# Hybrid decoder trunk: when a block's DMA transposes are issued and when its halves are joined

## The chip, the cores and the metric

The kernel runs on one core of one Trainium2 chip. The metric is device time in microseconds of one execution. A core has five engines that work side by side, each with its own queue of instructions: TensorE (PE in the profile; PEld is its loading of stationary operands), VectorE (DVE), ScalarE (ACT), GpSimd (POOL) and SyncE (SP). DMAs are issued here by SP, by POOL (those that add to what stands at their destination) and a few by ACT; sixteen DMA engines of the core carry them out.

## The reference

Two layers over 512 tokens of width 1024 in float32. Each has a SwiGLU feed-forward part (ffn) of width 2816, a token mixer (windowed attention beside a short convolution, not touched here), and a second ffn:

```python
x = x + 0.5 * swiglu(rms_norm(x, ffn1_norm[l]), ffn1_wg[l], ffn1_wu[l], ffn1_wd[l])
...
x = x + jnp.concatenate([attn_out, conv_out], axis=-1) @ w_out[l]
x = x + 0.5 * swiglu(rms_norm(x, ffn2_norm[l]), ffn2_wg[l], ffn2_wu[l], ffn2_wd[l])
...
def swiglu(h, w_gate, w_up, w_down):
    return (jax.nn.silu(h @ w_gate) * (h @ w_up)) @ w_down
```

A final RMSNorm follows.

## The kernel before

**Precision.** Every operand of a matmul is split into two halves of reduced precision, `hi` and `lo`; a product is made of three matmuls (hi by hi, lo by hi, hi by lo). For weights, `split` does this: ScalarE casts `raw` to `wh` (L214), VectorE subtracts to get `wl` (L215). There are three buffers each of `wh` and `wl`, and `need_split` runs two splits ahead of the matmuls.

**Pairs.** An ffn is a list of stages (`FIRST`, `INNER` or `LAST`). A stage "w" (`winograd2`) computes the gate and up products of 512 hidden columns, called a block here, with seven products in place of eight (a Strassen-like scheme, `CHAINS`). It has seven steps; each consumes two weight tiles of 512 KB and runs 24 matmuls of 128 x 512 (`stream`, L816). I call such a stage a pair and count its steps from 0 in the code, from the first in the text. In the first ffn the last such stage is a narrower form of 256 columns ("u", `winograd`). A pair needs ten weight tiles; four of them are sums of two matrices, loaded by SP and completed by an accumulating DMA of POOL (L209). There are eight buffers `raw` for 512 KB tiles, loaded ahead in the order of the plan; a load waits on SP's queue until its buffer is free, and everything behind it on that queue waits too.

**Share stages.** After the pairs, a stage "s" (`share`) multiplies the activations of two blocks by `wd`, again seven products for eight; an ffn has two such stages, and the block of its last pair, which is in neither, is turned on TensorE. In it POOL also sums two weight tiles by DMA (L281). In the very last ffn a closing stage "e" stands in place of the second share (its tiles end in `_e`).

**Crossing.** The activations `ups` leave a pair with tokens on the partitions, four tiles of 128 x 512 float32, and the share stage needs the hidden columns there. The blocks listed in `blocks` (four in each of the four ffn, sixteen in all) are turned by DMA: an object `Crossing` is put on the list `crossing` at the end of its pair, and its `step` is called once at the end of each step of the pairs that follow (`turns`). For each of four token tiles ScalarE copies the float32 words apart into their upper and lower 16-bit halves (`halves`, L1090), and SP issues a DMA transpose of 2-byte elements into `turned` (L1091). Later `join` (L1105) has ScalarE put the two halves together again, four copies of 128 x 1024 16-bit words, into `raw_a`, from which the operands of the share stage are made. A join needs all four transposes of its block. `join` stands behind the latest cast in ScalarE's order (`issue_after`).

When: with `n` the count of steps since the block was made, a block's transposes go at n = 0 to 3, one per step, and its joins at n = 8 and 9, two each, that is in the second and third step of the pair after the next. The last block of an ffn (`b == max(blocks)`) has `first = 3`: its transposes go in the fourth to seventh step of the last pair, and the first share stage joins it in its fourth step (`joined`). `turned` and `raw_a` come from a pool of four buffers (`g8`), `halves` from a pool of fourteen (`g2`).

The order on an engine's queue is the program's order, rearranged by a scheduler; the transposes share SP's queue with the weight loads (L197).

Of the kernel before, what the change touches and what calls it, by code (L numbers as in the profile page):

```python
# [25 lines left out]
NT = S // P  # L26
# [46 lines left out]
def trunk_kernel(  # L73
# [35 lines left out]
    def g2(name, dt=F32, shape=(P, S)):  # L109
        return work.tile(list(shape), dt, tag="g2", bufs=14, name=name)  # L110

    def g8(name, dt=F32R, shape=(P, 2, 2, S)):
        return work.tile(list(shape), dt, tag="g8", bufs=4, name=name)
# [778 lines left out]
    def ffn(norm, stages, after=None, late=None):  # L892
# [43 lines left out]
        def winograd(b, between):  # L936
# [9 lines left out]
            def keep(what, m, src):  # L946
                if m == 0:
                    kept[what] = g2(f"{what}_{name}", F32, (P, 2, H))
                nc.scalar.copy(kept[what][:, m, :], src)

            for step, (acc, operand, start) in enumerate(CHAINS):
                _, wh, wl = take_split()
                xh, xl = norm.forms[operand]
# [5 lines left out]
                for m in range(2):  # L959
# [27 lines left out]
                    if step == 6:  # L987
                        nc.scalar.activation(gate[:, t2], out, AF.Silu)
                        nc.vector.tensor_mul(up, up, gate)
                        split(hi[:, m, :], lo[:, m, :], up)  # L990
                turns(step)
                between(step)
            acts[b] = (hi, lo)

# [72 lines left out]
        class Crossing:  # L1067
# [2 lines left out]

            def __init__(self, b, name, ups):
                self.b, self.name, self.ups = b, name, ups

                self.first = 3 if b == max(blocks) else 0
                self.steps = 0
                self.to = None

# [3 lines left out]
            def step(self):  # L1081

                n = self.steps
                self.steps += 1
                t = n - self.first
                if t == 0:
                    self.to = g8(f"turned_{self.name}", U16, (P, 2, NT, S))
                if 0 <= t < NT:
                    halves = g2(f"halves{t}_{self.name}", U16, (P, 2, S))
                    nc.scalar.copy(halves, self.words(self.ups[t]))  # L1090
                    nc.sync.dma_start_transpose(  # L1091
                        self.to.rearrange("p a c s -> p (a c) s")[:, :, t * P : (t + 1) * P],
                        halves.rearrange("p a n -> p (a n)"),
                    )
                if n in (8, 9):
                    self.join(*((0, 1), (2, 3))[n - 8])
                return n == 9

            def join(self, *cs):

# [29 lines left out]
        blocks = [b + j for what, b in stages if what in "se" for j in (0, 2)]  # L1130
# [512 lines left out]
```

## Time and profile before

| | |
|---|---|
| median of 3 runs | 1681.74 us (1675.95 to 1684.97) |
| the profiled execution | 1688.44 us, its span 1686.6 us, granted TensorE clock 0.996 |
| VectorE, ScalarE busy in the span | 82%, 64% |
| mean DMA rate | 179 GB/s |
| transposes | 64 |

The span runs from the first to the last instruction. An engine's busy share is a mean over stages with different limits, so the prediction goes by stage. In lines of waits the name after the arrow is who ended the wait; a wait for several is put down to the one that came last.

### The profile page before, as it was taken

How to read it: one execution, taken by the hardware profiler on the slowest of the kernel's cores; microseconds unless marked ns; L12 is line 12 of the kernel's file. 1: busy time of each engine (PE TensorE's matmuls, PEld its weight loads, DVE VectorE, ACT ScalarE, POOL GpSimd, SP SyncE). 2: the span in 40 equal slices, each digit the busy share in tenths (PEclk: the TensorE clock that was granted, in tenths of full speed). 3: DMA queues.
4: the chain of work that ended last, by engine and by line, in shares of the span. 5: the costliest groups of instructions: out<-in, count | busy, mean ns of one | idle time of the engine just before them, and what ended most of it. 6: DMA issues, size and time to landing. Idle time of an engine off the chain costs nothing. (4 is left out here: it accounts for less than half of the span.)

```text
span 1686.6 us, 22112 instructions
## 1 busy us (share of the span) xinstructions
PE 1650.6 (98%) x8140; PEld 1389.9 (82%) x8140; DVE 1381.6 (82%) x1824; ACT 1073.0 (64%) x1425; POOL 212.4 (13%) x188
## 2 busy tenths in 40 slices
PE   9999999999999999989999999999999999999988
PEld 7888889988898878877888778878888988888766
DVE  7987679988899967778898667888788997678887
ACT  6446776466576667757466567764565766777645
POOL 0011111001111111111011111110012111111121
PEclk9999999999999999999999999999999999999999
DMA  8379997831497799898567999985125968998992
GB/s 251 88 189 204 239 215 191 199 88 52 126 226 166 186 191 240 212 169 218 174 138 188 191 216 215 197 222 170 50 63 140 223 138 212 216 216 206 209 252 74
DMA packets 260129, 301.92 MB, mean 179 GB/s; under 512 B 76652, under 2 KB 145332, under 8 KB 260020
## 3 DMA queue, kind: packets, MB, share of 16 engines
q1 hardware_dynamic: 219428, 218.04, 46.2%
q0 software_dynamic: 39872, 81.80, 29.0%
q8 instruction: 64, 1.05, 0.2%
q10 hardware_dynamic: 720, 0.66, 0.1%
q14 instruction: 45, 0.37, 0.1%
HBM read 262.71 MB, written 2.10 MB: 157 GB/s over the span
## 5 line engine op out<-in xcount | busy, mean ns | idle before, releaser
L214 ACT CAST wh<-raw 128x1024 fp32r<-128x1024 f32 (+1 forms) x491 | 511.3, 1046 | 453.2 <-PE x L816 101.4
L215 DVE TENSOR_TENSOR wl<-raw,wh 128x1024 fp32r<-128x1024 f32 (+1 forms) x491 | 593.8, 1219 | 188.7 <-ACT wh L214 187.8
L310 PE MATMUL acc<-xh,wh 128*128 128x512 f32 x424 | 165.8, 392 | 0.0
L311 PE MATMUL acc<-xl,wh 128*128 128x512 f32 x424 | 165.5, 390 | 0.0
L313 PE MATMUL acc<-xh,wl 128*128 128x512 f32 x416 | 162.2, 390 | 0.0
L209 POOL DMA_DIRECT2D raw<-in_ffn_wu_dram x39 | 48.9, 1254 | 403.1 <-DMA raw<-in_ffn_wu_dram 324.5
L311 PEld LDWEIGHTS acc<-xl,wh 128*128 128x128 f32 x424 | 79.7, 188 | 15.9 <-DVE xl L491 0.2
L310 PEld LDWEIGHTS acc<-xh,wh 128*128 128x128 f32 x424 | 79.8, 188 | 15.7
L313 PEld LDWEIGHTS acc<-xh,wl 128*128 128x128 f32 x416 | 78.1, 188 | 16.4
L1105 ACT COPY raw_a<-turned 128x1024 uint16<-128x1024 uint16 x64 | 84.1, 1361 | 0.0
L251 DVE TENSOR_TENSOR raw<-raw,raw 128x1024 f32<-128x1024 f32 x56 | 68.0, 1222 | 19.4 <-DMA raw<-in_ffn_wu_dram 17.3
L209 POOL DMA_DIRECT2D raw<-in_ffn_wg_dram x39 | 48.2, 1248 | 239.2 <-DMA raw<-in_ffn_wu_dram 135.1
L209 POOL DMA_DIRECT2D raw<-in_ffn_wd_dram x34 | 41.0, 1206 | 279.9 <-DMA raw<-in_ffn_wd_dram 139.1
L816 PE MATMUL w<-wl,fb21h 128*128 128x512 f32 x152 | 59.4, 391 | 3.8 <-DVE wl L215 3.8
L816 PE MATMUL x<-wh,ft1h 128*128 128x512 f32 x152 | 59.3, 390 | 1.4 <-ACT wh L214 1.4
L816 PE MATMUL x<-wl,ft1h 128*128 128x512 f32 x152 | 59.8, 394 | 0.8 <-DVE wl L215 0.8
L816 PE MATMUL y<-wl,ft3h 128*128 128x512 f32 x152 | 59.2, 390 | 0.4 <-DVE wl L215 0.4
L816 PE MATMUL w<-wh,fb21h 128*128 128x512 f32 x152 | 59.3, 390 | 0.0
L816 PE MATMUL x<-wh,ft1l 128*128 128x512 f32 x152 | 59.2, 390 | 0.0
L816 PE MATMUL y<-wh,ft3h 128*128 128x512 f32 x152 | 59.2, 390 | 0.0
L816 PE MATMUL x<-wh,ft2h 128*128 128x512 f32 x152 | 59.2, 390 | 0.0
L816 PE MATMUL w<-wh,fb21l 128*128 128x512 f32 x152 | 59.2, 389 | 0.0
(604 smaller groups left out, 4606.1 us busy)
## 6 DMA issues: line engine op xcount, KB each, us to landing
raw<-in_ffn_wu_dram SPq DMA_DIRECT2D x126, 512.0 KB, 4.9
raw<-in_ffn_wd_dram SPq DMA_DIRECT2D x105, 512.0 KB, 5.8
raw<-in_ffn_wg_dram SPq DMA_DIRECT2D x86, 512.0 KB, 5.0
raw<-in_ffn_wu_dram POOLq DMA_DIRECT2D x39, 512.0 KB, 9.7
raw<-in_ffn_wg_dram POOLq DMA_DIRECT2D x39, 512.0 KB, 6.1
raw<-in_w_in_dram SPq DMA_DIRECT2D x36, 512.0 KB, 3.7
raw<-in_ffn_wd_dram POOLq DMA_DIRECT2D x34, 512.0 KB, 8.7
raw<-raw POOLq DMA_DIRECT2D x21, 512.0 KB, 8.0
```

The lines of the kernel that those rows point to most:

```text
L209: nc.gpsimd.dma_start(out=r, in_=rows_of(*more), accum_op=ALU.add)
L214: cast = nc.scalar.copy(hi, raw)
L215: eng.tensor_sub(lo, raw, f32(hi))
L251: nc.vector.tensor_add(a11, a11, s1)
L310: nc.tensor.matmul(acc, hi[:, k, :], rhs[k][0], start=k == first, stop=False)
L311: nc.tensor.matmul(acc, hi[:, k, :], rhs[k][1], start=False, stop=False)
L313: nc.tensor.matmul(acc, lo[:, k, :], rhs[k][0], start=False, stop=k == last)
L816: nc.tensor.matmul(accs[u], x_[:, 2 * h + k, tok], w[:, k, :], start=start and h + k + i == 0, stop=h + k == 2 and i == 2, skip_group_chec ...
L1105: nc.scalar.copy(self.words(raws[self.b][:, c, :]), self.to[:, :, c, :])
```

## The change

The transposes of every block, the last one too, go in the first two steps of the next pair, two in each. A block that is not the last of its ffn is joined in the sixth and seventh step of that same pair, two copies in each; the last block is joined by the first share stage, as before. The attribute `first` goes. Nothing is computed differently, and the loads and splits keep their order among themselves but for two neighbouring loads in the last ffn.

```diff
             def __init__(self, b, name, ups):
                 self.b, self.name, self.ups = b, name, ups
-
-                self.first = 3 if b == max(blocks) else 0
                 self.steps = 0
                 self.to = None
...
                 n = self.steps
                 self.steps += 1
-                t = n - self.first
-                if t == 0:
+                if n == 0:
                     self.to = g8(f"turned_{self.name}", U16, (P, 2, NT, S))
-                if 0 <= t < NT:
+                for t in {0: (0, 1), 1: (2, 3)}.get(n, ()):
                     halves = g2(f"halves{t}_{self.name}", U16, (P, 2, S))
                     nc.scalar.copy(halves, self.words(self.ups[t]))
                     nc.sync.dma_start_transpose(
                         self.to.rearrange("p a c s -> p (a c) s")[:, :, t * P : (t + 1) * P],
                         halves.rearrange("p a n -> p (a n)"),
                     )
-                if n in (8, 9):
-                    self.join(*((0, 1), (2, 3))[n - 8])
-                return n == 9
+
+                if n in (5, 6) and self.b != max(blocks):
+                    self.join(*((0, 1), (2, 3))[n - 5])
+                    return n == 6
+                return False
```

On SP's queue the new order within a pair is: transpose, load, transpose, load, transpose, load, transpose, load; before it was transpose, three loads, transpose, and so on.

## The prediction

> **What bounds the kernel now.** I read the page first, for who is busy, then a table of busy time by stage, then the waits inside the stages that come out too long, then the DMAs in flight there.
>
> ```profile
> span 1686.6 us, 22112 instructions
> PE 1650.6 (98%) x8140; PEld 1389.9 (82%) x8140; DVE 1381.6 (82%) x1824; ACT 1073.0 (64%) x1425; POOL 212.4 (13%) x188
> ```
>
> TensorE sets the time; only its 36 us of idleness, and what it runs slowly, can be won. The table by stage (start and end, length, busy time of each engine with its count, granted clock, DMA share, GB/s) shows where. The boundaries are the first matmuls of the stages.
>
> ```profile
> 580.11:618.19 38.08, 38.08 (x170) 31.54 (x168) 27.88 (x29) 23.77 (x29) 4.84 (x4) 1.00 1.00 186
> 618.19:658.17 39.98, 38.48 (x170) 31.37 (x168) 27.52 (x29) 27.68 (x33) 4.81 (x4) 1.00 0.94 241
> 658.17:696.32 38.15, 38.15 (x169) 31.46 (x168) 27.61 (x29) 27.90 (x33) 4.81 (x4) 1.00 0.93 219
> 696.32:734.40 38.08, 38.08 (x169) 31.54 (x168) 34.41 (x36) 31.72 (x37) 4.82 (x4) 1.00 0.88 161
> 734.40:781.17 46.77, 40.79 (x170) 32.41 (x168) 31.41 (x32) 27.98 (x32) 6.65 (x6) 0.96 0.99 217
> ...
> 956.41:1000.38 43.97, 39.31 (x169) 31.23 (x168) 27.52 (x29) 27.88 (x33) 4.81 (x4) 1.00 1.01 222
> ...
> 1038.54:1077.18 38.64, 38.38 (x169) 31.45 (x168) 35.22 (x36) 31.81 (x37) 4.84 (x4) 1.00 0.87 185
> 1077.18:1117.34 40.16, 38.65 (x169) 31.38 (x168) 31.32 (x32) 28.01 (x32) 6.64 (x6) 1.00 0.96 230
> ...
> 1570.36:1614.46 44.10, 41.08 (x185) 32.84 (x184) 36.41 (x41) 26.92 (x30) 9.17 (x9) 1.00 1.06 263
> ```
>
> A pair of 168 matmuls takes 38.08 us undisturbed (first row). The exceptions: two pairs, each the third of its ffn, are 1.90 and 5.89 us too long, one last pair 0.56. The share stage after a last pair has as many matmuls and is 8.69 and 2.08 too long; the third one also runs 16 transposes, eight in 0.87 us by the chain of waits, which leaves 44.10 - 38.08 - 1.74 = 4.28. One more wait stands at the start of the closing stage:
>
> ```profile
> 1583.98 0.87 PE at L1054 x8
> ...
> 1628.17 0.77 PE L816 MATMUL x_e<-wh,ft2h_e 128*128 128x512 f32 x1 [5.38 <-DVE bias L1259]
> ...
> 1632.07 0.39 PE L816 MATMUL x_e<-wh,ft2h_e 128*128 128x512 f32 x1
> ```
>
> 5.38 us idle, and after it nine matmuls from 1628.17 to 1632.07 in 3.90 us where nine take 9 x 0.227 = 2.04 (38.08 / 168): 7.24 in all. Together 1.90 + 5.89 + 0.56 + 8.69 + 2.08 + 4.28 + 7.24 = 30.6 us. What is late there? For the first of them, by the DMAs in flight:
>
> ```profile
> 604.64 3.25 SPq L1091 DMA_TRANSPOSE turned<-halves  x1
> 603.53 1.20 POOL L209 DMA_DIRECT2D raw<-in_ffn_wu_dram  x1 [19.55 <-DMA raw<-in_ffn_wu_dram]
> 606.19 1.21 POOL L209 DMA_DIRECT2D raw<-in_ffn_wu_dram  x1 [1.46 <-DMA raw<-in_ffn_wu_dram]
> ...
> raw<-in_ffn_wg_dram SPq DMA_DIRECT2D x86, 512.0 KB, 5.0
> raw<-in_ffn_wg_dram SPq DMA_DIRECT2D x2, 512.0 KB, 11.5
> turned<-halves SPq DMA_TRANSPOSE x1, 14.7
> ACT wh L214 <- DMA raw<-in_ffn_wg_dram: 3.6, 1, 3.6
> ```
>
> The block's fourth transpose left between two accumulating loads of POOL and took 14.7 us to land; the two weight loads issued beside it took 11.5 at the median (5.0 over the whole run, the row above), and at 618 to 628 us ScalarE waited 3.6 us for such a load, with TensorE behind it. Transposes that meet no accumulating load are quick; those that do are slow (landing of those issued at 666 to 679, at 720 to 739, at 964 to 974 us):
>
> ```profile
> DMA to landing us min/median/max: 2.7/3.1/3.4
> DMA to landing us min/median/max: 11.2/17.8/19.6
> DMA to landing us min/median/max: 7.9/9.7/11.5
> ```
>
> The second row is the last block's four, just ahead of the share stage that is 8.69 too long; the third lies in the pair that is 5.89 too long.
>
> **The change part by part.** It removes and adds no instruction: 64 transposes, 64 halves copies and 64 joins stay.
>
> ```profile
> L1091 SPq DMA_TRANSPOSE turned<-halves x64: 1231/1233/6863, 124.9 to 1578.3; - x64
> L1090 ACT COPY halves<-u x32: 1027/1044/1076, 123.8 to 1556.4; 128x1024 uint16<-128x1024 uint16 x32
> L1105 ACT COPY raw_a<-turned 128x1024 uint16<-128x1024 uint16 x64 | 84.1, 1361 | 0.0
> ```
>
> *Transposes of the twelve earlier blocks.* In the pair from 580.11 the fourth left at 604.64, 24.5 us in, 1.1 us after the accumulating load. In the new order all four stand among the first four loads of the SP queue in the pair, the last just ahead of the fourth. Their copies follow the first step (5.44 us) and the second (10.9): with two silus of 0.6 and two copies of 1.04 after it, the last is ready some 14 to 15 us in (estimate), 8 us before the first accumulating load at 23.4 us in. A transpose alone lands in 3.1 us, so it is gone by then. I take the 1.90, 5.89 and 0.56 as won: 8.3 us. Bounds: 0 if the meeting only moves, 8.35.
>
> *The same for the last block.* Its transposes leave in the first two steps of the last pair rather than from the fourth on: some 8 to 15 us into 696.32 to 734.40, not 720 to 739. The DMA share of this stage is only 0.88, so there is room. The share stages lose 8.69 + 2.08 + 4.28 = 15.05; part of it is the second half of the stage, whose loads wait for buffers behind the sum on POOL. I take 0.8 of it, 12 us; bounds 0 and 15.05.
>
> *Closing stage.* Its 7.24 us end in loads that queue at a DMA share of 1.06; they start earlier when the share stage's loads do, but TensorE comes earlier too. I take half, 3.6; bounds 0 and 7.24.
>
> *Against it, in the first ffn:*
>
> ```profile
> 235.25 1.19 POOL L209 DMA_DIRECT2D raw<-in_ffn_wd_dram  x1 [11.70 <-DMA raw<-in_ffn_wd_dram]
> 240.88 1.20 POOL L209 DMA_DIRECT2D raw<-in_ffn_wd_dram  x1 [4.45 <-DMA raw<-in_ffn_wd_dram]
> ...
> 247.97 3.94 SPq L1091 DMA_TRANSPOSE turned<-halves  x2
> ```
>
> The last pair there is the narrow form. Its transposes go from 248 and later to about 239 to 246 us, onto these two accumulating loads. One such meeting cost 1.9 in the row at 618.19 and, with a second, 5.89: I take 2; bounds 0 and 5.9.
>
> *SP queue.* Three transposes now pass ahead of loads that they stood behind, 3 x 1.23 us of issue. The delayed loads are the end of the same pair's weights and the next pair's first, needed 15 us and more later by TensorE: nothing, and 3.7 us a pair if that cover were gone.
>
> *ScalarE.* The joins move from the second and third step to the sixth and seventh, two per step, between the casts there:
>
> ```profile
> 1488.63 1.05 ACT L214 CAST wh<-raw 128x1024 fp32r<-128x1024 f32 x1 [1.67 <-PE y L816]
> 1491.35 1.05 ACT L214 CAST wh<-raw 128x1024 fp32r<-128x1024 f32 x1 [1.67 <-PE x L816]
> 1492.93 0.60 ACT L1038 ACTIVATE gate<-x 128x512 f32<-128x512 f32 x1 [0.53 <-PE x L816]
> 1494.07 1.06 ACT L214 CAST wh<-raw 128x1024 fp32r<-128x1024 f32 x1 [0.54 <-PE x L816]
> 1495.03 0.58 ACT L1038 ACTIVATE gate<-x 128x512 f32<-128x512 f32 x1
> 1496.64 1.23 DVE L251 TENSOR_TENSOR raw<-raw,raw 128x1024 f32<-128x1024 f32 x1 [1.77 <-DMA raw<-in_ffn_wu_dram]
> 1498.39 1.22 DVE L215 TENSOR_TENSOR wl<-raw,wh 128x1024 fp32r<-128x1024 f32 x1
> ```
>
> The idle times in brackets are the room. In the new order two joins of 1.36 precede the first cast, which ends at 1490.7; the second is on time, to 1492.4; join to 1493.8, gate to 1494.4, join to 1495.7, gate to 1496.3, and the cast of 1494.07 ends at 1497.4. Its wl starts in the trace only at 1498.39, since VectorE stands behind a sum (L251) that waits for an accumulating load, so the wl is no later than now: done at 1499.6, where TensorE's second step begins at 1494.09 + 5.44 = 1499.5 and wants wl with its third matmul, at 1500.0. That 0.4 us is what is late next: behind this wl queue the following wl, then TensorE. Nothing by this count; I take 2 us over the twelve blocks, bounds 0 and 12 (one us each). A join also waits for the last landing: 15 + 3.1 us in, wanted at 29.
>
> Sum: 8.3 + 12 + 3.6 - 2 - 2 = 20 us off the profiled execution's 1688.44 (span 1686.6, the rest around it): 1668.4. The median before is 1681.74, 6.7 lower, so the runs shown have fewer of these waits; with the won waits scaled by (30.6 - 6.7) / 30.6 it is 1681.7 - (23.9 x 0.78 - 4) = 1667.
>
> **Rivals.** *The meeting moves to the head of the pair (slower).* The other two accumulating loads of a pair are issued near its start, and now two transposes follow at once:
>
> ```profile
> 658.97 1.20 POOL L209 DMA_DIRECT2D raw<-in_ffn_wg_dram  x1 [8.57 <-DVE p L1039]
> 661.08 1.20 POOL L209 DMA_DIRECT2D raw<-in_ffn_wg_dram  x1 [0.90 <-DVE raw L251]
> ...
> 962.79 2.48 POOL L209 DMA_DIRECT2D raw<-in_ffn_wg_dram  x2 [17.12 <-DMA raw<-in_ffn_wu_dram]
> ```
>
> For it: where these loads went out at 962.79, the transpose issued at 964 to 965 met them and landed in 7.9 us or more (third landing row). Against: at 658.97 and 661.08 they were in time, the transposes issued from 666 on land in 3.1, and without the meeting at 24 us into the pair before, the loads come earlier. The price is what a pair lost by one meeting, 1.90, or half of 5.89, which had two, 2.9; at 2.3 and 16 blocks 37 us against 24 won: 1688 + 13 = 1701. It decides once more than ten blocks meet (24 / 2.3).
>
> The Trainium skill, DMA: Bandwidth & Descriptors, section Queues, rings and completion order, has each DMA engine take turns between queues a packet at a time. By it a transpose of many small packets is held up for as long as any accumulating load runs, which is this rival's mechanism; the trace has both outcomes.
>
> *ScalarE and VectorE become the bound:* the 0.4 us is gone and each of twelve blocks costs one us more than I took: 1667 + 10 = 1677. For it: 0.4 us is little. Against: the joins leave the second and third step, where two of them already follow one cast, and the pair from 658.17 lost 0.07.
>
> *It is volume, not the meeting:* the share and closing stages have DMA shares of 0.99 and 1.06 and are late however the transposes lie; the time stays, 1682. Against: the pair from 580.11, at 1.00, runs without a wait.
>
> The Trainium skill, Advanced Engine Details and Errata, section X-Bar Transpose (TRN2), says that a transposing DMA is as fast as an ordinary one. By it the change only moves ordinary traffic and the sum is 0. The trace agrees for a transpose alone (3.1 us) and not for one beside an accumulating load (14.7).
>
> **How the numbers follow.** Forecast 0.60, meeting at the head 0.21, ScalarE and VectorE 0.09, volume 0.10. Predicted 1667. If everything is won and nothing paid, 1681.7 - 30.6 x 0.78 = 1658, as from the profiled time (1688.4 - 30.6); 1653 is that less the spread of the runs before (1675.95 to 1684.97, 4 or 5 us either side). Above, the two middle rivals at 1677 and 1682, nearly all of them, give 1683; the 0.21 at 1701 stays out, but for its mildest cases. The forecast's own range is 1658 to 1674. Half a per cent (8.4 us, about what can be told from no change) puts the bounds at 1673.3 and 1690.1: faster 0.60, same 0.19 (the two middle rivals), slower 0.21.
>
> **What would show it.** Right: no transpose with a landing over 10 us outside the first ffn; the stage rows at 38.1 us for all pairs and under 41 for the share stages; TensorE's idle sum under 20 us. Wrong: landings of 8 us and more for the first two transposes of a block, accumulating loads there over 10 us; ScalarE's joins followed by TensorE waits on wh or wl in a pair's second step; or share stages unchanged in length.

## The result, and the profile after

| | before | after |
|---|---|---|
| median | 1682.63 us of 4 runs (1675.95 to 1684.97) | 1658.91 us of 4 runs (1658.15 to 1661.39) |
| the profiled execution | 1688.44 us | 1659.43 us |

The ratio of after to before is 0.9868, 95% interval 0.9838 to 0.9898: faster by 1.3%. The forecast was 1667 us in a range of 1653 to 1683. In the experiments below, one run of `e2_joins` (of six) and four of `e3_last` (of twelve, its profiled one among them) took over 1.5% longer than the fastest run of the same kernel, count as slow, and are left out of the medians and ratios.

The profile page of after, the span and the busy time of each engine:

```profile
span 1657.6 us, 22095 instructions
PE 1642.2 (99%) x8140; PEld 1389.2 (84%) x8140; DVE 1380.6 (83%) x1824; ACT 1075.1 (65%) x1425; POOL 212.4 (13%) x188
```

The counts on each engine are those of before. TensorE is idle for 1657.6 - 1642.2 = 15.4 us of the span, where it was 36. The table of busy time by stage of after, its columns those of the prediction's (start and end, length, each engine's busy time, granted clock, DMA share, GB/s):

```profile
616.84:654.92 38.08, 38.08 (x170) 31.53 (x168) 27.70 (x29) 28.09 (x34) 4.84 (x4) 1.00 0.94 221
...
693.00:731.08 38.08, 38.08 (x170) 31.53 (x168) 35.43 (x37) 29.27 (x36) 4.21 (x4) 1.00 0.92 207
731.08:769.77 38.69, 38.38 (x169) 31.45 (x168) 30.09 (x31) 27.50 (x31) 6.62 (x6) 1.00 0.83 205
945.03:983.11 38.08, 38.08 (x169) 31.54 (x168) 27.70 (x29) 28.11 (x34) 4.47 (x4) 1.00 0.91 220
1021.19:1059.27 38.08, 38.08 (x169) 31.54 (x168) 35.43 (x37) 29.29 (x36) 4.24 (x4) 1.00 0.91 213
1059.27:1097.99 38.72, 38.40 (x169) 31.46 (x168) 30.10 (x31) 27.55 (x31) 6.58 (x6) 1.00 0.88 225
1550.86:1590.73 39.87, 39.87 (x185) 33.19 (x184) 35.52 (x40) 26.31 (x29) 9.89 (x9) 1.00 1.02 266
...
1590.73:1657.60 66.87, 57.77 (x271) 48.10 (x269) 57.30 (x81) 38.21 (x57) 11.86 (x9) 0.98 0.48 126
0.00:307.09 307.09, 301.79 (x1557) 256.52 (x1558) 248.89 (x295) 192.54 (x241) 34.90 (x38) 0.99 0.79 198
```

Every pair that was too long before now takes the undisturbed 38.08. Set beside the rows of before, the 29.0 us of span (1686.6 - 1657.6) came from these stages. The closing stage and the stretch up to the end of the first two share stages have these rows in before's table:

```profile
1614.46:1686.60 72.14, 59.57 (x271) 49.46 (x269) 57.88 (x81) 38.24 (x57) 12.66 (x9) 0.93 0.52 130
...
0.00:308.37 308.37, 302.23 (x1556) 256.17 (x1557) 248.66 (x295) 192.45 (x241) 34.82 (x38) 1.00 0.81 197
```

| where | before to after, us | won |
|---|---|---|
| pairs | 1.90 + 5.89 + 0.56 over 38.08, now 0 | 8.4 |
| first share stages | 46.77, 40.16, 44.10 to 38.69, 38.72, 39.87 | 13.8 |
| closing stage | 72.14 to 66.87 | 5.3 |
| the first ffn | 308.37 to 307.09 | 1.3 |
| sum | | 28.8 of 29.0 |

The wait at the start of the closing stage is there still, but shorter. TensorE's timeline of after at that place (start, duration, what ran, and in brackets the idle time before it with what ended it):

```profile
1600.89 0.47 PE L816 MATMUL x_e<-wh,ft2h_e 128*128 128x512 f32 x1 [1.84 <-DVE bias L1258]
...
1603.04 0.39 PE L816 MATMUL x_e<-wh,ft2h_e 128*128 128x512 f32 x1
```

1.84 us where it was 5.38; nine matmuls later TensorE stands at 1603.04, 2.15 us on, against 3.90 before and 2.04 at full pace. The slow matmuls went with the long wait: 7.24 - (1.84 + 0.11) = 5.29, which is the stage's 72.14 - 66.87 = 5.27 us.

The transposes of after, with issue times, and their time to landing; first the whole run, then the four in the pair from 616.84:

```profile
L1088 SPq DMA_TRANSPOSE turned<-halves x64: 1237/1239/4118, 124.2 to 1527.9; - x64
DMA to landing us min/median/max: 2.7/5.0/7.7
...
L1088 SPq DMA_TRANSPOSE turned<-halves x4: 1237/1238/2048, 624.8 to 632.0; - x4
DMA to landing us min/median/max: 2.7/5.3/6.1
```

And POOL's timeline of after, its accumulating loads in that pair:

```profile
617.36 2.49 POOL L209 DMA_DIRECT2D raw<-in_ffn_wg_dram  x2 [11.78 <-DVE wl L215]
642.71 2.44 POOL L209 DMA_DIRECT2D raw<-in_ffn_wu_dram  x2 [22.86 <-DMA raw<-in_ffn_wu_dram]
```

The four transposes lie in the gap between POOL's two visits: the first goes 624.8 - 617.4 = 7.4 us after the first pair of loads, the last, at 632.0, 10.7 us ahead of the second. None of those whose landing the trace shows (52 of the 64) takes more than 7.7 us, where the slowest took 19.6 (of 53 that show it).

### The profile page after: what moved, and what is told of

It is laid out like the page before. It is cut to its first block, busy times and chain, and to the rows that moved or that the text cites. A ratio compares the mean times of both kernels' runs of the same rounds, so it can differ in the third digit from the quotient of the medians.

```text
span 1657.6 us, 22095 instructions
## 1 busy us (share of the span) xinstructions
PE 1642.2 (99%) x8140; PEld 1389.2 (84%) x8140; DVE 1380.6 (83%) x1824; ACT 1075.1 (65%) x1425; POOL 212.4 (13%) x188
## 2 busy tenths in 40 slices
DMA packets 260129, 301.92 MB, mean 182 GB/s; under 512 B 76652, under 2 KB 145332, under 8 KB 260020
## 3 DMA queue, kind: packets, MB, share of 16 engines
q0 software_dynamic: 39872, 81.80, 28.5%
## 4 chain that ended last, share of the span: by engine, by line
PE 93%; DVE 3%; ACT 2%; DMA 1%; issue 1%; SPq 0%; POOL 0%; ACTq 0%; DVEq 0%; POOLq 0%
PE x L816 25%; PE y L816 12%; PE acc L310 8%; PE acc L311 8%; PE acc L313 8%; PE w L816 6%; PE x_s L816 5%; PE x_m L801 3%; PE y_s L816 3%; PE x_s L801 2%; PE y_s L801 1%; PE y_m L801 1%; DVE wl L215 1%; PE x_e L816 1%; PE acc L696 1%
## 5 line engine op out<-in xcount | busy, mean ns | idle before, releaser
L209 POOL DMA_DIRECT2D raw<-in_ffn_wu_dram x39 | 49.0, 1256 | 393.6 <-DMA raw<-in_ffn_wu_dram 227.1
L209 POOL DMA_DIRECT2D raw<-in_ffn_wg_dram x39 | 48.3, 1265 | 227.3 <-DMA raw<-in_ffn_wu_dram 97.2
L209 POOL DMA_DIRECT2D raw<-in_ffn_wd_dram x34 | 41.0, 1207 | 265.8 <-DMA raw<-in_ffn_wd_dram 173.7
L816 PE MATMUL x<-wl,ft2h 128*128 128x512 f32 x152 | 59.1, 389 | 0.0
```

The source lines that it names most:

```text
L209: nc.gpsimd.dma_start(out=r, in_=rows_of(*more), accum_op=ALU.add)
L816: nc.tensor.matmul(accs[u], x_[:, 2 * h + k, tok], w[:, k, :], start=start and h + k + i == 0, stop=h + k == 2 and i == 2, skip_group_chec ...
```

## The experiments

Times are medians. Ratios are to the kernel before on the same chip, whose medians were 1677 to 1680 us in every group of runs; the first four rows ran on another chip than the rest, so rows of the two groups are best compared by their ratios. "The twelve" are the three earlier blocks of each of the four ffn, "the last" its last block.

| run | the twelve | the last | median, us | ratio (95%) |
|---|---|---|---|---|
| `e1_early12` | early transposes, old joins | as before | 1679.54 | 1.0002 (0.9979 to 1.0024) |
| `e2_joins` | old transposes, early joins | as before | 1709.40 | 1.0190 (1.0151 to 1.0229) |
| `e3_last` | one transpose per step, early joins | early | 1686.67 | 1.0046 (1.0014 to 1.0077) |
| `e4_fourth` | after, 4th transpose in the 4th step | the same | 1707.60 | 1.0162 (1.0123 to 1.0200) |
| `e10_third` | after, 4th transpose in the 3rd step | the same | 1658.09 | 0.9887 (0.9864 to 0.9910) |
| `e6_zero` | after, all four in the 1st step | the same | 1658.58 | 0.9861 (0.9836 to 0.9885) |
| `e5_again` | after | after | 1658.04 | 0.9864 (0.9836 to 0.9891) |
| `e7_lastlate` | after | as before | 1677.27 | 0.9983 (0.9956 to 1.0011) |
| `e12_lastalone` | as before | after | 1666.34 | 0.9905 (0.9882 to 0.9929) |
| `e9_lasttwo` | third block as after | after | 1664.32 | 0.9925 (0.9902 to 0.9948) |
| `e8_plain` | as before, POOL does not add | as before | 1662.10 | 0.9883 (0.9857 to 0.9908) |
| `e11_fourth_plain` | `e4_fourth`, POOL does not add | the same | 1669.24 | 0.9941 (0.9916 to 0.9967) |

### The twelve's transposes alone

```diff
-                if 0 <= t < NT:
+                for t in (((0, 1), (2, 3), (), ()) if not self.first else ((0,), (1,), (2,), (3,)))[t] if 0 <= t < NT else ():
```

> The kernel before, with only the transposes of the twelve earlier blocks moved to the first two steps; all joins and the last blocks' transposes stay where they were. Meeting theory (a transpose is slow, and delays the weight loads, when it is in flight beside POOL's accumulating loads): no transpose of the twelve lands later than 7 us, all pairs take 38.1 us, the first share stages stay long (over 40 us each, 46.8 in the trace of before), time about 1676. ScalarE theory (the joins in the second and third step of a pair are what held TensorE up): pairs still lose, time as before, 1682. Volume theory (the DMA engines are simply full): 1682.

No gain: ratio 1.0002, where the meeting theory expected about 1676 us; no change is what the other two theories expected. The meetings of the twelve are gone, as these four transposes show, issued at 627.4 to 634.8 in the pair that was 1.90 too long before:

```profile
DMA to landing us min/median/max: 2.7/3.7/4.6
```

But something took their place, and the pairs still lose, as the ScalarE theory had it. The stage table of this kernel has no pair of 44 us, and small losses in some eight pairs:

```profile
619.47:658.33 38.86, 38.39 (x170) 31.44 (x168) 27.52 (x29) 27.88 (x33) 4.81 (x4) 1.00 0.90 208
658.33:697.17 38.84, 38.38 (x169) 31.44 (x168) 26.90 (x29) 27.88 (x33) 4.81 (x4) 1.00 0.92 220
```

The waits of TensorE in those last two pairs name VectorE's `wl` and nothing else; ScalarE's timeline shows why it is late:

```profile
PE y L816 <- DVE wl L215: 0.9, 2, 0.5
```

```profile
629.16 1.36 ACT L1105 COPY raw_a<-turned 128x1024 uint16<-128x1024 uint16 x1
...
630.91 1.34 ACT L1105 COPY raw_a<-turned 128x1024 uint16<-128x1024 uint16 x1
632.12 1.03 ACT L1090 COPY halves<-p 128x1024 uint16<-128x1024 uint16 x1
...
633.59 1.03 ACT L1090 COPY halves<-p 128x1024 uint16<-128x1024 uint16 x1
634.53 1.99 ACT L214 CAST wh<-raw 128x1024 fp32r<-128x1024 f32 x2
```

Two old joins and two new halves copies now stand in the same step, back to back: from 629.16 ScalarE does no cast until 634.53, 5.4 us, a whole step of TensorE (38.08 / 7 = 5.44). The trace is that of the fastest of the twelve runs (1673.26 us): in it two of the three first share stages take only 38.70 and 39.87 us, and one 43.04, although the last blocks' transposes are where they were and the expectation had all three over 40. How long a share stage gets with late transposes is thus not fixed.

So the joins of the earlier block have to leave the second and third step if the copies come in. That half of the change is there to make room.

### The joins alone

```diff
-                if n in (8, 9):
-                    self.join(*((0, 1), (2, 3))[n - 8])
-                return n == 9
+                if n in (5, 6) and self.b != max(blocks):
+                    self.join(*((0, 1), (2, 3))[n - 5])
+                    return n == 6
+                return False
```

> The kernel before, with only the joins of the twelve earlier blocks moved to the sixth and seventh step of the next pair; all transposes stay where they were. Meeting theory: fourth transposes still land after 10 us and more in some pairs, the share stages stay long, time within 5 us of 1682. ScalarE theory: most of the gain is here, 1659 to 1665.

Both theories missed: slower by 1.9%, some 32 us. The waits of TensorE are mostly on ScalarE, and the page's group of joins, whose last column is the idle time of ScalarE just before them, tells what ScalarE stood for:

```profile
PE x L816 <- ACT wh L214: 15.7, 4, 6.2
PE w_s L816 <- ACT wh L214: 6.6, 3, 2.3
PE x L965 <- ACT wh L214: 5.9, 1, 5.9
```

```profile
L1106 ACT COPY raw_a<-turned 128x1024 uint16<-128x1024 uint16 x64 | 83.6, 1350 | 45.5 <-DMA turned<-halves 45.5
```

A join needs all four transposes of its block. With the fourth still in the fourth step and meeting the accumulating loads, it lands after the join's turn has come, and ScalarE, which runs in order, stands for 45.5 us in all, with the casts of the weights behind it.

### One transpose late, with early joins

`e3_last` gives the twelve one transpose per step again; `e4_fourth` delays only the fourth, `e10_third` delays it by one step, `e6_zero` puts all four in the first step. The diffs are to the kernel after, the one removed line and then the line of each in this order:

```diff
-                for t in {0: (0, 1), 1: (2, 3)}.get(n, ()):
+                for t in ({0: (0, 1), 1: (2, 3)} if self.b == max(blocks) else {i: (i,) for i in range(NT)}).get(n, ()):
...
+                for t in {0: (0, 1), 1: (2,), 3: (3,)}.get(n, ()):
...
+                for t in {0: (0, 1), 1: (2,), 2: (3,)}.get(n, ()):
...
+                for t in {0: (0, 1, 2, 3)}.get(n, ()):
```

> The changed kernel, but the twelve earlier blocks send one transpose per step over four steps, as before; joins and the last blocks' transposes as changed. Meeting theory: share stages at 38 to 39.5 us, and one or two pairs lose 2 to 6 us to a fourth transpose that lands after 10 us and more: 1663 to 1669. Volume theory: nothing is gained anywhere in particular, 1675 to 1682. ScalarE theory: 1659, as the changed kernel.

> The changed kernel, with only the fourth transpose of each block put back from the second step to the fourth, next to POOL's accumulating loads. Meeting theory: fourth transposes land after 9 to 15 us in several blocks, the loads beside them too, and one to three pairs lose 2 to 6 us: 1662 to 1670. Volume theory: one transpose of four moved by 11 us changes nothing, 1659. ScalarE theory: 1659.

> The changed kernel, with only the fourth transpose one step later, in the third step, some 4 us ahead of POOL's next accumulating loads. Meeting theory: it lands within 7 us and the time is the changed kernel's, 1657 to 1661. If any transpose later than the second step costs: 1665 and more.

> The changed kernel, with all four transposes of a block in the first step. Meeting theory: all four are gone before POOL's next accumulating loads as well, so the time is within 3 us of the changed kernel's, unless the first two steps are still near POOL's earlier pair of loads (landings over 8 us there, 1665 and more). ScalarE theory: four copies of 1.04 us in a row hold up the casts and each pair loses 0.5 to 1 us: 1666 to 1675.

`e4_fourth` shows the whole mechanism in one place. POOL's timeline, the transpose between its two loads with who waited for it, and ScalarE's timeline, all of this kernel:

```profile
988.00 1.20 POOL L209 DMA_DIRECT2D raw<-in_ffn_wu_dram  x1 [19.86 <-DMA raw<-in_ffn_wu_dram]
990.81 1.20 POOL L209 DMA_DIRECT2D raw<-in_ffn_wu_dram  x1 [1.60 <-DMA raw<-in_ffn_wu_dram]
```

```profile
L1088 SPq DMA_TRANSPOSE turned<-halves x1: 4352/4352/4352, 989.1 to 989.1; - x1
...
  ACT raw_a L1104: 10.3, 1
```

```profile
994.48 1.05 ACT L214 CAST wh<-raw 128x1024 fp32r<-128x1024 f32 x1 [1.67 <-PE y L816]
1005.82 2.51 ACT L1104 COPY raw_a<-turned 128x1024 uint16<-128x1024 uint16 x2 [10.29 <-DMA turned<-halves]
1008.21 1.98 ACT L214 CAST wh<-raw 128x1024 fp32r<-128x1024 f32 x2
```

The transpose leaves at 989.1 between the loads of 988.0 and 990.8; the join that needs it starts only at 1005.8, 16.7 us later, after 10.3 us of standstill, and two casts come 10 us late. Over the run ScalarE stands 69.6 us so, and TensorE pays: 49 us more than the kernel after (1707.6 against 1658.0; 50 by the ratios), where the expectation allowed 12. The meeting was foreseen, the queue behind the join was not.

In the third step (`e10_third`, 1658.09) or all in the first (`e6_zero`, 1658.58) the time is that of after: neither the exact step nor four copies in a row on ScalarE matter, as long as the fourth is gone before POOL's second visit. Landings are at most 9.9 and 6.4 us; the 9.9, over the 7 that was expected, lies in the narrow last pair of the first ffn and costs nothing that the time shows. `e3_last` missed all three expectations: it is slower than the kernel before by 0.5%, and than `e5_again` by 1.8% by the ratios. The same standstill is the likely reason, since its joins are early and its fourth transposes late; this is argued, not shown.

### The last block

```diff
-                if n == 0:
+                if n == (3 if self.b == max(blocks) else 0):
...
-                for t in {0: (0, 1), 1: (2, 3)}.get(n, ()):
+                for t in ({0: (0, 1), 1: (2, 3)} if self.b != max(blocks) else {3 + i: (i,) for i in range(NT)}).get(n, ()):
```

> The changed kernel, but with the last block of each ffn sent in the fourth to seventh step, as before. Meeting theory: all pairs at 38.1 us, the first share stage of the three later ffn 2 to 9 us too long: 1663 to 1673. If the share stages had been long for another reason: 1659, as the changed kernel.

> The changed kernel once more, on the chip of the next three: 20 to 27 us below the kernel before by every theory; it is the yardstick for them.

The same chip gave 1658.04 with the last block early and 1677.27 with it late: 19.2 us, of the 21.3 that all parts are worth there. The stage table of `e7_lastlate` (the three first share stages) and the landing of three transposes issued at 712 to 722 in that last pair:

```profile
725.97:768.23 42.26, 39.29 (x169) 31.17 (x168) 31.24 (x32) 28.03 (x32) 6.65 (x6) 1.00 1.01 231
1057.68:1100.31 42.63, 39.85 (x169) 31.07 (x168) 31.30 (x32) 28.00 (x32) 6.64 (x6) 1.00 0.93 225
1553.16:1595.33 42.17, 40.91 (x186) 32.83 (x185) 36.47 (x41) 26.90 (x30) 9.07 (x8) 1.00 1.04 275
```

```profile
DMA to landing us min/median/max: 10.5/15.7/17.6
```

All pairs of that table are at 38.08, the share stages 3.6, 3.9 and 2.3 us longer than after's. The median is 4 us above the range that the meeting theory gave, and the trace, of the second fastest of twelve runs (1670.22 us), shows less than the 19.2 us: the three share stages and 6.2 in the closing stage (73.07 us against 66.87).

How late transposes hold up TensorE shows on SP's queue. Here are SP's timeline of `e7_lastlate` from 712.42, ScalarE's first wait for weights in the share stage from 725.97, and, in the second fence, its counterpart in the kernel before, in the share stage from 734.40:

```profile
712.42 15.51 SPq L1088 DMA_TRANSPOSE turned<-halves  x3
728.03 1.56 SPq L197 DMA_DIRECT2D raw<-in_ffn_wd_dram  x3
733.84 1.05 ACT L214 CAST wh<-raw 128x1024 fp32r<-128x1024 f32 x1 [5.41 <-DMA raw<-in_ffn_wd_dram]
```

```profile
745.61 1.04 ACT L214 CAST wh<-raw 128x1024 fp32r<-128x1024 f32 x1 [8.76 <-DMA raw<-in_ffn_wd_dram]
```

A transpose occupies the queue for 1.2 us at the median; these three occupy it for 15.5. The weight loads behind them leave as soon as they are through, at 728.03, 2 us into the share stage; the first lands in 5.7 us, no later than such loads do over the run of before (5.8 at the median), and ScalarE has stood for 5.41 us. In before two transposes hold the queue for 9.0 us from 722.47, and the load behind them, at 731.59, also lands late, after 13.9 us. So what holds up the weights is the queue of SP as well as the landing of the loads, of which the prediction named only the second. In after ScalarE waits for no load in this stage. `e9_lasttwo` and `e12_lastalone` ask the opposite: how much is left with only the last two blocks, or only the last one, in the new order.

The first is a diff to the kernel after, the second to the kernel before:

```diff
+                self.early = b in sorted(blocks)[2:]
...
-                for t in {0: (0, 1), 1: (2, 3)}.get(n, ()):
+                for t in ({0: (0, 1), 1: (2, 3)} if self.early else {i: (i,) for i in range(NT)}).get(n, ()):
...
-                if n in (5, 6) and self.b != max(blocks):
-                    self.join(*((0, 1), (2, 3))[n - 5])
-                    return n == 6
+                j = 5 if self.early else 8
+                if n in (j, j + 1) and self.b != max(blocks):
+                    self.join(*((0, 1), (2, 3))[n - j])
+                    return n == j + 1
```

```diff
-                self.first = 3 if b == max(blocks) else 0
+                self.last = b == max(blocks)
...
-                t = n - self.first
-                if t == 0:
+                if n == 0:
...
-                if 0 <= t < NT:
+                for t in ({0: (0, 1), 1: (2, 3)} if self.last else {i: (i,) for i in range(NT)}).get(n, ()):
```

> The changed order for the last two blocks of each ffn alone (the last one early needs a free buffer, so the one before it is joined early too); the first two blocks of each ffn as before, one transpose per step and joins in the next pair but one. If the gain is the last blocks' transposes leaving the share stages: 1659 to 1666, share stages at 38.7 to 39.9 us, pairs of the middle losing 0 to 6 us. If the gain comes from all blocks alike: half of it, 1667 to 1671. If early joins are what matters: 1667 or more.

> The kernel before, in which only the last block of each feed-forward part is turned in the first two steps of the last pair, two per step; the twelve earlier blocks keep their order. Two theories of how the parts of the change add up. (1) The last block's move pays by itself, since it takes the transposes out of the accumulating loads ahead of the share stages: of the 19 us that it is worth beside the changed order of the twelve, most is there without it, time 1660 to 1667, the first share stages within 1 us of 38.7, 38.7 and 39.9 in the profile. (2) It pays only with the third block's early transposes and joins, which otherwise stand beside it in the last pair: ScalarE is crowded there by four copies and two or four joins, the share stages stay late, time 1671 to 1679.

Both keep most of the gain (1664.32 and 1666.34, ratios 0.9925 and 0.9905, not told apart). In `e12_lastalone` the share stages are 39.84, 39.82 and 40.35, two of them just past the one us that the first theory allowed, and the meetings of the twelve are still there, as one pair of its stage table shows:

```profile
729.78:769.62 39.84, 38.99 (x169) 31.30 (x168) 30.29 (x31) 31.76 (x35) 6.62 (x6) 1.00 0.83 201
944.78:989.46 44.68, 40.34 (x170) 32.53 (x169) 29.88 (x30) 27.89 (x33) 4.81 (x4) 0.96 0.97 226
```

So by ratios, at 1680 us: the twelve alone -2.9 us (`e7_lastlate`; its interval holds 0), the last alone -16.0, both -22.8. The sum of the two parts, -18.9, is not told from the whole. But the twelve's two halves don't add up at all: transposes alone 0, joins alone +32, together -2.9.

### POOL's loads without the adding

In these two, POOL's second load of a summed tile (L209) overwrites the first instead of adding to it. These sums of weights are left out, with the same bytes and the same instructions. L209 issues 120 of POOL's 156 DMAs; the other 36, among them the sum in the share stage (L281), still add.

```diff
-                nc.gpsimd.dma_start(out=r, in_=rows_of(*more), accum_op=ALU.add)
+                nc.gpsimd.dma_start(out=r, in_=rows_of(*more))
```

> The kernel before, where POOL's second load of a summed weight tile overwrites the first in place of being added to it: the sums of weights are left out, bytes from memory and queues are the same. If it is the adding that slows transposes: all land within 7 us, pairs at 38.1 us, share stages under 40, time 1660 to 1668. If it is the sharing of the DMA engines with POOL's queue as such: landings of 10 us and more remain, 1672 to 1685.

> The variant that puts the fourth transpose into the fourth step (1707.6 us), with POOL's second load of a summed tile overwriting in place of adding: the sums of weights are left out. If the adding, or the DMA time that it takes, is what slows the transposes and with them the joins: 1657 to 1665, ScalarE waiting under 10 us for transposes (69.6 before). If it is the mere presence of POOL's queue: 1690 to 1710.

The kernel before without the adding takes 1662.10, 17.2 us less than with it and 4.1 more than `e5_again` on the same chip. So most of what the change wins is lost only where these loads add. But the expectation for the adding was also that all transposes land within 7 us, and that failed: landings reach 14.6 us, and seven of the 53 that the trace shows are over 10, against ten before. So transposes beside POOL's loads are late here too; without the adding it costs TensorE little. With the fourth transpose late, ScalarE's standstill before the joins falls from 69.6 to the 26.5 us of this row of `e11_fourth_plain`'s page:

```profile
L1104 ACT COPY raw_a<-turned 128x1024 uint16<-128x1024 uint16 x64 | 83.8, 1353 | 26.5 <-DMA turned<-halves 26.5
```

and its time from 1707.6 to 1669.2. That is 38 of the 49 us; the other 11 stay although nothing adds, so this came out between the two expectations. What adding costs the DMA engines shows in the page's rows for POOL's queue (packets, MB, share of 16 engines' span), of before and of `e8_plain`:

```profile
q0 software_dynamic: 39872, 81.80, 29.0%
```

```profile
q0 software_dynamic: 24000, 81.80, 18.4%
```

The adding itself and the DMA time that it takes both go in these runs, and POOL's loads are themselves done sooner. Which of these makes a late transpose dear was not tried apart, and stays open.

## Why the prediction was right

*What bounds the kernel.* Right. TensorE's waits came from weight loads that were late beside slow transposes, and with the landings down from at most 19.6 to 7.7 us nearly all of them are gone. The signs named for it came: no landing over 10 us, share stages under 41 us, TensorE idle for 15.4 us. The reading that a transpose is slow when it meets an accumulating load was too coarse, though. In the trace of before the six fourth transposes issued 1.3 to 1.4 us ahead of POOL's second visit land in 5.9 to 7.2 us (the one at 683.13, for instance, in 6.2, with POOL's load at 684.39), the three issued 0.8 to 1.2 us behind its first load in 14.4 to 14.9 (landings are those that the trace shows; of the last block's four behind 720, three). Being 1.3 us ahead of the visit was enough. And a late landing is not always paid for: behind the one of 14.9, issued at 141.52, neither that pair nor the next is longer than 38.16 us. Of the 30.6 us of losses counted in before, 28.8 - 1.3 = 27.5 were won, and 1.3 in the first ffn besides.

*The twelve earlier blocks, 8.3.* In the profiled execution the size is right (8.4, all of these pairs at 38.08), and with the last block early the runs come near it: 6.9 us by the ratios of `e5_again` and `e12_lastalone`, whose intervals overlap slightly. With the last block late the twelve win 2.9, not told from nothing. And the step gave the gain to the transposes alone, while `e1_early12` shows that these alone win nothing: without the joins' move the crowded ScalarE takes it back. The joins' move, which the sum counted only as a cost, is what makes it worth something; that the size came out is luck in this respect.

*The last block, 12.* Right, 13.8 in the profile. Three us were kept back for the second half of the stage, behind the sum on POOL; little of that was there, and the stages ended at 38.7, 38.7 and 39.9, under the 41 that the prediction asked for. That this part is the larger one is shown twice, by `e7_lastlate` (19.2 us lost without it) and `e12_lastalone` (16.0 won with it alone).

*The closing stage, 3.6.* Mis-sized: 5.3. The loads came earlier by more than TensorE did: by SP's timelines weight loads go out again 14.0 us into the share stage ahead of it (1564.88 - 1550.86), where it was 23.1 (1593.43 - 1570.36), 9 us sooner, while the closing stage starts 4.2 us sooner (44.10 to 39.87).

*The first ffn, -2.* Mis-sized: no new meeting was paid; the stretch is 1.3 us shorter.

*ScalarE and VectorE, -2.* Mis-sized: nothing was paid. The order of ScalarE's work in the last steps was right; two joins do delay the casts. ScalarE's and VectorE's timelines of after, at the end of a pair that ends at 654.92:

```profile
653.13 1.35 ACT L1104 COPY raw_a<-turned 128x1024 uint16<-128x1024 uint16 x1
...
654.83 1.36 ACT L1104 COPY raw_a<-turned 128x1024 uint16<-128x1024 uint16 x1
...
656.54 2.13 ACT L214 CAST wh<-raw 128x1024 fp32r<-128x1024 f32 x2
```

```profile
655.90 1.23 DVE L251 TENSOR_TENSOR raw<-raw,raw 128x1024 f32<-128x1024 f32 x1 [0.20 <-DMA raw<-in_ffn_wu_dram]
...
657.64 1.22 DVE L215 TENSOR_TENSOR wl<-raw,wh 128x1024 fp32r<-128x1024 f32 x1
```

The prediction put `wl` at 1498.39 - 1494.09 = 4.3 us into the pair, behind a sum that waited 1.77 us for an accumulating load. Here that sum waits 0.20 and `wl` starts 2.7 us in, done at 658.86, 1.5 us ahead of the second step at 654.92 + 5.44, or 2.0 ahead of its third matmul, from where the prediction counted its 0.4. In the pair that the prediction used, which starts at 1474.70 now, it is the same: `wl` starts 2.7 us in. The margin that seemed to be 0.4 us was itself set by the late load, and grew when the load came in time.

*The sum.* 20 us predicted for the profiled execution, 29.0 measured: 1.8 more from the share stages, 1.7 from the closing stage, and 3.3 and 2 from the two costs that were not there. The pairs give 0.1. All these errors point one way, and the measured time is the 1658 that the prediction worked out for everything won and nothing paid. The scaling to the median held: 0.78 x 28.8 = 22.5, against 1681.74 - 1658.91 = 22.8 us.

*The rivals.* That the meeting moves to the head of the pair: refuted, the transposes follow POOL's first visit by some 7 us and land in 7.7 at most. The Trainium skill, DMA: Bandwidth & Descriptors, section Queues, rings and completion order, has queues take turns a packet at a time; by that rule a transpose is held up only while such a load runs. The trace of after agrees, with 2.7 to 6.1 us in the pair from 616.84, between the loads. That ScalarE and VectorE become the bound: not in the kernel after, but TensorE waits on them in both halves of it, in `e1_early12` because ScalarE is crowded, in `e2_joins` because it stands and waits for a transpose. That it is volume: refuted, since before, after and `e7_lastlate` all move 301.92 MB, and after is 22.8 us faster than before and 19.2 faster than `e7_lastlate`. DMA time does matter, as `e8_plain` shows, but the place of the transposes decides whether it is paid for. By the Trainium skill, Advanced Engine Details and Errata, section X-Bar Transpose (TRN2), a transposing DMA is as fast as an ordinary one. The 23.7 us between the medians of the result refute what the prediction made of that sentence, a sum of 0, and not the sentence: beside an accumulating load ordinary loads were late too, 11.5 us against 5.0, and a transpose alone takes 3.1.

## What to carry to other kernels

When a transfer is slow in some places and quick in others, list what is in flight beside it before counting bytes: here four small transposes had to be issued in the gap between two visits of another queue, and which step exactly did not matter. Look also at how long the transfer holds the queue that issues it, since everything behind it there leaves late. Before a consumer is moved earlier on an engine that runs in order, ask when its input lands at the worst, since all that stands behind it waits too; a join moved ahead of its transposes cost 32 us, the same join behind them nothing. Undo each half of a change by itself: one half may win nothing, the other lose, and both be needed.

## What the hardware showed unexpectedly

Adding DMAs are dear. The 81.80 MB of POOL's queue take 29.0% of the DMA engines' time when all 156 DMAs add and 18.4% when 120 of them do not, in 39872 packets against 24000. By these shares a DMA that adds takes about twice the time of one that does not: an estimate, with 29.0% of 1686.6 us spread evenly over 156, which is 3.1 us of all sixteen engines each, and what 36 such leave of 18.4% of 1658.9 us spread over 120, which is 1.6.

Even with these loads not adding, a transpose beside them can be slow: in `e8_plain` landings still reach 14.6 us, five of the seven over 10 us at last blocks, and the time is only 4 us above that of after.

The kernel after is also steadier: its runs spread over 3 to 4 us (1656.69 to 1660.37 in `e5_again`), those of before over 8 to 24 (1664.48 to 1688.96 beside it, though of more runs). It goes with the last blocks: with these late and the twelve early the spread is 13 us (`e1_early12`, `e7_lastlate`), with the last alone early 6 (`e12_lastalone`). That fits meetings that come out another way from run to run, though no run shows it directly.
